# Differential attention with the matrix engine's order written out by hand, and the projections spread over all its items

## The chip, the cores and the metric

One core of one Trainium2 chip runs the kernel. The metric is device time in microseconds (us) from start to end of one execution; lower is better. A core has a matrix engine (TensorE, PE in the rows; PEld is its weight load), VectorE (DVE), ScalarE (ACT), GpSimd (POOL) and SyncE (SP), which here issues the weight transfers. Each engine works through its own queue in order and waits on semaphores for the others.

## What is computed

The reference is a four-layer block followed by a two-layer block over 256 tokens of width 1024. The change lies in layer 1 of the first block, a differential attention with 8 heads over 256 latent and 256 context tokens:

```python
def diff_attend(q1, q2, k1, k2, v, lam):
    scale = DIFF_HEAD_DIM ** -0.5
    s1 = jnp.einsum("bqhd,bkhd->bhqk", q1, k1).astype(jnp.float32) * scale
    s2 = jnp.einsum("bqhd,bkhd->bhqk", q2, k2).astype(jnp.float32) * scale
    p = jax.nn.softmax(s1, axis=-1) - lam * jax.nn.softmax(s2, axis=-1)
    return jnp.einsum("bhqk,bkhe->bqhe", p.astype(v.dtype), v)
...
q, k, v = jnp.split(h @ w_qkv, 3, axis=-1)      # rotary positions on the latent q and k
...
return (rms_norm(o, subln_g) * (1 - lam_init)).reshape(b, s, D_MODEL) @ w_o
```

Latent queries see all 512 keys, context queries the 256 context keys. A residual addition, a norm and an MLP of hidden width 4096 follow, as in every layer.

## The kernel before, in words

All products run on TensorE in pieces of a high and a low part, so one projection product is three matmuls. `loadw` fetches 256 columns of a weight (1 MB), and ScalarE (L306) and VectorE (L307) split them into two halves of high and low parts; five such halves fit at a time.

The attention of `diff` is cut into 24 items (h, it): for each of 8 heads two blocks of 128 latent queries (it = 0, 1) and one item with both context blocks (it = 2). An item has four parts:

- `scores`: ScalarE and VectorE split the queries (L396, L397); TensorE makes both score maps (L1227); VectorE takes maxima (L1231) and negates them (L1233); ScalarE takes the exponentials (L1238); VectorE combines the two maps into the probabilities p (L1242, L1243, L1247). From the second head on, the keys of the next head are split in the item with it = 2.
- `values`: TensorE transposes p (L1258), ScalarE copies the transpose out (L1260, tile `pt`), TensorE multiplies it with the values (L1267), ScalarE copies and squares the result (L1269, L1272). With it = 2 VectorE then computes the head's norm (L415 to L421) and scales the output (L1281).
- `finish`, once for each head: TensorE transposes the output (L1288), ScalarE and VectorE split it (L1290, L1291).
- fill: `qkv(g)` makes keys, queries and values of the head pair g in 8 steps, first four over 512 columns (`linear`, L324, L325, L327), then four over 256 columns (`val`, L1199 to L1201), each of 24 matmuls. `wo` is half of the output projection as `linear_k` with 8 steps of 12 matmuls over 512 columns (L351 to L353); step k needs the finished head k. The other half follows in `tail`.

The program traces, for each item, `scores` of this item, then steps of the fill, then `values` of the item before (`pipe_feed`). The fill of pair g+1 runs during the six items of pair g, so the last pair's six items have no projections left and take `wo` in the portions of DIFF_WO. The order in which each engine issues is not the traced one: the framework's scheduler reorders all instructions by readiness in its own model, with the traced order as priority.

`rows_add(rate)` adds to a counter and, whenever it passes 1, traces one more unit of the modulation weights of later layers: a transfer of 1 MB and two or four VectorE reductions over it (L588). RATES[1] is its rate for each item of `diff`; RATES[2] and RATES[4] are those of the MLPs of layers 1 and 2. The units come in a fixed sequence, so those that `diff` does not take are taken by these MLPs.

Of the kernel before, what the change touches and what calls it, by code (L numbers as in the profile page):

```python
# [17 lines left out]
P = 128  # L18
# [208 lines left out]
}  # L227
NDT = 5
AHEAD = 200
RATES = (0.35, 0.13, 0.6, 0.0, 0.3)  # L230
START = 12
LEAD = 2
DIFF_WO = (0, 1, 1, 1, 1, 0, 3)
DIFF_FIN = ((0, 1), (2, 3), (4,), (5,), (6,), ())
ORDER = [2, 5, 8, 11, 0, 1, 3, 4, 6, 7, 9, 10] + list(range(12, 24))
SCHED = ((6, 0), (6, 0), (6, 0), (6, 0), (6, 1), (4, 3), (0, 2), (0, 2))
BOTH = [(0, 0, NL), (1, NL, NF)]
# [4 lines left out]
class Body:  # L242
# [27 lines left out]
    def mm(self, cols=512):  # L270
        return self.ps.tile([P, 512], F32, tag="mm", name=self.nm("mm"))
# [67 lines left out]
    def linear_k(self, aps, xs, n, evac, m0=0):  # L339


        mm = self.nc.tensor.matmul
        ns = n if isinstance(n, list) else [n] * 2 * len(aps)
        ws = [self.loadw(ap, 8, 256) for ap in aps]
        pss = [self.mm() for _ in range(2 * len(aps))]
        for k in range(8):
            for i, ps in enumerate(pss):
                w = ws[i // 2]
                c0 = (i % 2) * P
                n = ns[i]  # L350
                mm(ps[:, :n], w(0, k, c0, c0 + P), xs[k][0][:, :n], start=k == 0, stop=False)  # L351
                mm(ps[:, :n], w(0, k, c0, c0 + P), xs[k][1][:, :n], start=False, stop=False)
                mm(ps[:, :n], w(1, k, c0, c0 + P), xs[k][0][:, :n], start=False, stop=k == 7)  # L353
            if k < 7:
                yield
        for i, ps in enumerate(pss):
            evac(m0 + i, ps)
        yield

    def pipe_begin(self, a, b, lag):  # L360

        self.pp = (a, b, lag, [])
# [795 lines left out]
    def diff(self, mod, nxt):  # L1158
        nc = self.nc
# [49 lines left out]
        def keys(h):  # L1209
            kx[h] = self.split(ks.pop(h)[:, :512])  # L1210

        def scores(h, it):


            self.rows_add(RATES[1])
            nq, k0, nk = (1, 0, 512) if it < 2 else (2, 256, 256)
            if h == 0 and it == 0:
                keys(0)
            q = self.split(qs[h][:, it * P:(it + nq) * P])
            if it == 2 and h < 7:  # L1220
                keys(h + 1)
            s = [self.aux(), self.aux()]
            for c in range(nq):
                for n_, (a, b) in enumerate(((0, 0), (0, 1), (1, 0))):
                    for i in range(2):
                        r = slice(64 * i, 64 * i + 64)
                        nc.tensor.matmul(s[i][:, c * nk:c * nk + nk], q[a][r, c * P:c * P + P],  # L1227
                                         kx[h][b][r, k0:k0 + nk], start=n_ == 0, stop=n_ == 2)
            mx, nm, ac, r = [self.sm(4)[:, :2 * nq] for _ in range(4)]
            for i in range(2):  # L1230
                nc.vector.tensor_reduce(out=mx[:, i * nq:i * nq + nq], in_=s[i].rearrange("p (c k) -> p c k", c=nq),  # L1231
                                        axis=AX.X, op=ALU.max)
            nc.vector.tensor_scalar(out=nm, in0=mx, scalar1=-scale, scalar2=None, op0=ALU.mult)  # L1233
            es = [self.g() for _ in range(2)]
            c0 = 4 * h + it
            for i in (1, 0):
                for c in range(nq):
                    nc.scalar.activation(es[i][:, c * nk:c * nk + nk], s[i][:, c * nk:c * nk + nk], AF.Exp,  # L1238
                                         bias=nm[:, i * nq + c:i * nq + c + 1], scale=scale,
                                         accum_out=ac[:, c:c + 1] if i else dac[:, c0 + c:c0 + c + 1])  # L1240

            nc.vector.reciprocal(r[:, :nq], ac[:, :nq])  # L1242
            nc.vector.scalar_tensor_tensor(out=r[:, :nq], in0=r[:, :nq], scalar=nlam, in1=dac[:, c0:c0 + nq],  # L1243
                                           op0=ALU.mult, op1=ALU.mult)
            for c in range(nq):
                sl = slice(c * nk, c * nk + nk)
                nc.vector.scalar_tensor_tensor(out=es[0][:, sl], in0=es[1][:, sl], scalar=r[:, c:c + 1],  # L1247
                                               in1=es[0][:, sl], op0=ALU.mult, op1=ALU.add)
            return es[0]

        def values(h, it, p):


            g, e0 = h // 2, (h % 2) * P
            nq = 1 if it < 2 else 2
            ps = self.aux()
            for j in range(4):
                nc.tensor.transpose(ps[:, j * P:j * P + P], p[:, j * P:j * P + P], self.ident)  # L1258
            pt = self.g()[:, :512]
            nc.scalar.copy(pt, ps)  # L1260
            if it == 0:
                of[h] = self.g()[:, :512]
            o = self.aux()
            nj = 4 // nq
            for j in range(4):
                jk = j if it < 2 else 2 + j % 2
                nc.tensor.matmul(o[:, j // nj * P:j // nj * P + P], pt[:, j * P:j * P + P],  # L1267
                                 vs[g, jk // 2][:, jk % 2, e0:e0 + P], start=j % nj == 0, stop=j % nj == nj - 1)
            nc.scalar.copy(of[h][:, it * P:(it + nq) * P], o[:, :nq * P])  # L1269
            sq = self.tp.tile([P, 512], F32, tag="sq", name=self.nm("sq"), bufs=2)  # L1270
            for c in range(nq):
                nc.scalar.activation(sq[:, c * P:c * P + P], o[:, c * P:c * P + P], AF.Square,  # L1272
                                     accum_out=dss[:, 4 * h + it + c:4 * h + it + c + 1])
            if it == 2:
                hc = slice(4 * h, 4 * h + 4)
                ep = self.sm(4)
                nc.vector.scalar_tensor_tensor(out=ep, in0=dac[:, hc], scalar=EPS, in1=dac[:, hc],
                                               op0=ALU.mult, op1=ALU.mult)
                self.rstd_of(dss[:, hc], dr[:, hc], 1.0 / P, ep)
                o3 = of[h].rearrange("p (q e) -> p q e", e=P)  # L1280
                nc.vector.tensor_tensor(out=o3, in0=o3, in1=dr[:, hc].unsqueeze(2).to_broadcast([P, 4, P]), op=ALU.mult)  # L1281

        def finish(h):

            ps = self.aux()
            o = of.pop(h)
            for j in range(4):
                nc.tensor.transpose(ps[:, j * P:j * P + P], o[:, j * P:j * P + P], self.ident)  # L1288
            hi, lo = self.pair(512)
            nc.scalar.activation(hi, ps, AF.Copy, scale=sg)  # L1290
            nc.vector.scalar_tensor_tensor(out=lo, in0=ps, scalar=sg, in1=hi.bitcast(F32), op0=ALU.mult,  # L1291
                                           op1=ALU.subtract)
            os_[h] = (hi, lo)
# [4 lines left out]
        def qkv(g):  # L1298
            yield from kq(g)
            yield from val(g)  # L1300
# [9 lines left out]
        hs = self.nb.hs  # L1310
        yield from val(0)
        wo = self.linear_k([I["diff_w"][12], I["diff_w"][13]], os_, 512, out)
        for g in range(4):
            items = [(h, it) for h in (2 * g, 2 * g + 1) for it in range(3)]
            fill = qkv(g + 1) if g < 3 else wo
            if g == 0:
                self.pipe_begin(scores, values, 1)
            if g < 3:
                self.pipe_feed(items, fill, 4 / 3)
                self.drain(fill)  # L1320
            else:
                for i, it in enumerate(items):
                    self.pipe_feed([it], wo, DIFF_WO[i])
                    for h in DIFF_FIN[i]:
                        finish(h)
            yield
        self.pipe_end(wo, 0)
        for _ in range(DIFF_WO[6]):
            next(wo)
        finish(7)  # L1330
        self.drain(wo)
        yield from self.tail([I["diff_w"][12 + u] for u in (2, 3)], [os_[h] for h in range(8)], out, 4)

    def mla(self, streams, mod, nxt):
# [87 lines left out]
        def scores(h, qi):  # L1422
            self.rows_add(RATES[3])
            s = self.aux()
# [123 lines left out]
    def first(self):  # L1548
        nc, I = self.nc, self.I
        with ExitStack() as ctx:  # L1550
# [23 lines left out]
            for l in range(DEPTH):  # L1574
# [38 lines left out]
                def ev(m, ps, st=None, mod=mod, streams=streams, n=n, l=l):  # L1613
# [5 lines left out]
                    elif st:  # L1619
                        self.final_add(m)  # L1620

                mlp = self.mlp_gen([I["mlp_w1"][l, u] for u in range(16)], w2, n, ev, nxt_mix if l < 3 else None)
                self.run(mlp, (RATES[0], RATES[2], RATES[4], 0)[l], START,
                         self.mod_units([20, 21, 22, 23], mod) if l == 0 else iter(()))
# [613 lines left out]
```

## Time and profile before

| what | value |
|---|---|
| median of 3 runs | 2950.53 us (2950.01 to 2952.84) |
| the profiled execution | 2948.07 us |
| its span, first to last instruction | 2946.3 us |
| TensorE busy | 2863.0 us, 97% of the span, 20316 matmuls |
| VectorE busy | 2153.2 us, 73% |
| ScalarE busy | 1489.9 us, 51% |
| mean granted TensorE clock | 0.991 |

The page's busy share of TensorE counts the modelled duration of pipelined matmuls, so a share near 100% says that one always was in flight, not that they followed each other as closely as they can. How close they came is read from the distance of their starts.

### The profile page before, as it was taken

The numbers are of one execution on the slowest core, as the hardware profiler recorded it, in microseconds if no ns is written. First come the engines' busy times: TensorE is split into PE (matmuls) and PEld (weight loads), VectorE is DVE, ScalarE is ACT, GpSimd is POOL, SyncE is SP. The second block draws the span as 40 slices with busy tenths as digits, with TensorE's granted clock in tenths as the row PEclk, the third lists the DMA queues.
The fourth block names the chain that finished last, engine by engine and source line by source line (L and its number), as shares of the span: only waits on it lengthen the run. The fifth ranks groups of instructions, "written<-read, shape, count | busy, mean of one in ns | idle before, by whom it ended". The sixth has DMA issues, their size and how long they took to land.

```text
span 2946.3 us, 51090 instructions
## 1 busy us (share of the span) xinstructions
PE 2863.0 (97%) x20316; PEld 2593.5 (88%) x20316; DVE 2153.2 (73%) x4707; ACT 1489.9 (51%) x2941; POOL 18.0 (1%) x66
## 2 busy tenths in 40 slices
PE   8999999998999999999999999999999999999999
PEld 6788889886888888599999999988999999989999
DVE  5597667775986667677756789886666799886765
ACT  5433323554432334855555567655554567655553
POOL 1000000000000000000000000000000000000000
PEclk9999999999999999999999999999999999999999
DMA  9454443320375553145525534333444444333553
GB/s 343 172 200 159 170 160 135 115 87 15 129 284 214 205 196 108 43 169 205 199 99 191 184 138 160 132 115 115 146 172 173 146 156 144 129 116 130 185 186 129
DMA packets 70366, 460.81 MB, mean 156 GB/s; under 512 B 7792, under 2 KB 9840, under 8 KB 16752
## 3 DMA queue, kind: packets, MB, share of 16 engines
q1 hardware_dynamic: 69984, 456.51, 43.6%
q8 instruction: 160, 2.62, 0.4%
q10 hardware_dynamic: 144, 1.05, 0.1%
q14 instruction: 78, 0.64, 0.1%
HBM read 456.47 MB, written 1.05 MB: 155 GB/s over the span
## 4 chain that ended last, share of the span: by engine, by line
PE 85%; DVE 8%; ACT 4%; DMA 1%; issue 1%; ACTq 0%; SPq 0%; DVEq 0%
PE mm L324 23%; PE mm L325 23%; PE mm L327 22%; DVE wlo L307 2%; ACT whi L306 1%; PE mm L675 1%; PE mm L674 1%; PE mm L676 1%; PE aux L1267 1%; PE mm L745 1%; PE aux L545 1%; PE mm L746 1%; PE mm L744 1%; DVE t L1701 1%; PE aux L1227 1%
## 5 line engine op out<-in xcount | busy, mean ns | idle before, releaser
L324 PE MATMUL mm<-g,whi 128*128 128x256 f32 (+3 forms) x5008 | 1406.9, 310 | 12.9 <-DVE t L1701 6.0
L325 PE MATMUL mm<-g,whi 128*128 128x256 f32 (+3 forms) x5008 | 1400.4, 308 | 0.5 <-DVE g L397 0.5
L306 ACT CAST whi<-raw 128x1024 fp32r<-128x1024 f32 (+2 forms) x670 | 697.5, 1048 | 821.0 <-PE mm L325 723.7
L324 PEld LDWEIGHTS mm<-g,whi 128*128 128x128 f32 x5008 | 941.6, 188 | 75.6 <-issue 15.7
L325 PEld LDWEIGHTS mm<-g,whi 128*128 128x128 f32 x5008 | 941.3, 188 | 51.7 <-issue 3.1
L307 DVE TENSOR_TENSOR wlo<-raw,whi 128x1024 fp32r<-128x1024 f32 (+2 forms) x670 | 809.5, 1210 | 122.0 <-ACT whi L306 65.7
L327 PE MATMUL mm<-g,wlo 128*128 128x256 f32 (+3 forms) x5008 | 835.2, 308 | 0.0
L327 PEld LDWEIGHTS mm<-g,wlo 128*128 128x128 f32 x5008 | 712.8, 188 | 47.0 <-issue 0.7
L588 DVE CUSTOM_DVE_ANT_0 junk<-raw,silu_b 128x1024 bf16<-128x1024 f32 x208 | 253.8, 1220 | 46.8 <-DMA raw<-in_mod_wT 44.9
L607 DVE SCALAR_TENSOR_TENSOR x<-mm,mod,x 128x256 f32<-128x256 f32 x216 | 98.3, 479 | 129.1 <-PE mm L327 125.4
L769 DVE TENSOR_TENSOR y<-mm,rb 128x256 f32<-128x256 f32 (+1 forms) x144 | 61.3, 427 | 89.8 <-PE mm L327 68.5
L846 DVE TENSOR_TENSOR g<-t,g 128x256 fp32r<-128x256 f32 (+2 forms) x192 | 98.5, 514 | 4.2
L843 ACT ACTIVATE t<-t 128x256 f32<-128x256 f32 (+2 forms) x192 | 94.0, 491 | 8.0 <-DVE g L846 2.9
L1701 DVE SCALAR_TENSOR_TENSOR t<-mm,cwh,t 128x270 f32<-128x270 f32 (+2 forms) x192 | 91.9, 490 | 2.7 <-ACT t L1698 2.4
L2195 DVE TENSOR_TENSOR x<-x,mm 128x272 f32<-128x272 f32 (+1 forms) x64 | 27.5, 429 | 81.0 <-PE mm L327 81.0
L675 PE MATMUL mm<-g,whi 128*128 128x256 f32 x240 | 66.7, 287 | 1.7 <-DVE g L643 1.6
L676 PE MATMUL mm<-g,wlo 128*128 128x256 f32 x240 | 65.5, 282 | 0.0
L841 ACT ACTIVATE t<-mm 128x512 f32<-128x512 f32 x64 | 37.9, 600 | 53.7 <-PE mm L327 53.6
L845 DVE CAST g<-t 128x256 fp32r<-128x256 f32 (+2 forms) x192 | 64.0, 334 | 1.3 <-ACT t L843 0.9
L674 PE MATMUL mm<-g,whi 128*128 128x256 f32 x240 | 60.7, 285 | 2.6 <-ACT g L642 2.6
L744 PE MATMUL mm<-g,whi 128*128 128x258 f32 (+2 forms) x192 | 54.5, 287 | 1.0 <-ACT g L716 0.7
L745 PE MATMUL mm<-g,whi 128*128 128x258 f32 (+2 forms) x192 | 54.7, 286 | 0.3 <-DVE g L717 0.3
(409 smaller groups left out, 3270.9 us busy)
## 6 DMA issues: line engine op xcount, KB each, us to landing
raw<-in_mlp_w SPq DMA_DIRECT2D x128, 1024.0 KB, 4.9
raw<-in_w_in SPq DMA_DIRECT2D x76, 1024.0 KB, 4.9
raw<-in_mod_wT SPq DMA_DIRECT2D x72, 1024.0 KB, 4.9
raw<-in_w_up SPq DMA_DIRECT2D x32, 1024.0 KB, 4.8
raw<-in_w_dn SPq DMA_DIRECT2D x32, 1024.0 KB, 4.8
raw<-in_diff_w SPq DMA_DIRECT2D x16, 1024.0 KB, 4.8
raw<-in_w_sd SPq DMA_DIRECT2D x16, 1024.0 KB, 4.8
raw<-in_mod_w SPq DMA_DIRECT2D x13, 1024.0 KB, 5.3
```

The source lines that it names most:

```text
L306: nc.scalar.copy(hi, v)
L307: nc.vector.tensor_tensor(out=lo, in0=v, in1=hi.bitcast(F32), op=ALU.subtract)
L324: mm(ps, w(0, k, c0, c1), xs[k][0], start=first and k == 0, stop=False)
L325: mm(ps, w(0, k, c0, c1), xs[k][1], start=False, stop=False)
L327: mm(ps, w(1, k, c0, c1), xs[k][0], start=False, stop=last and k == n - 1)
L588: nc.vector.tensor_tensor_reduce(out=self.junk, in0=r[:, D * j:D * j + D], in1=self.silu_b[:, D * s:D * s + D], scale=1.0, scalar=0.0, op0 ...
L607: self.nc.vector.scalar_tensor_tensor(out=self.x[m][:, c0:c1], in0=ps[:, c0:c1], scalar=mod[:, gc * 8 + m, s:s + 1], in1=self.x[m][:, c0:c ...
L675: mm(pss[i][:, c0:c1], w(0, k, o, o + P), l, start=False, stop=False)
L676: mm(pss[i][:, c0:c1], w(1, k, o, o + P), h, start=False, stop=k == 7)
L843: nc.scalar.activation(s[:, :n], t[:, :n], AF.Square)
L846: nc.vector.tensor_tensor(out=lo, in0=s[:, :n], in1=hi.bitcast(F32), op=ALU.subtract)
L1701: nc.vector.scalar_tensor_tensor(out=t[:, sft:L2], in0=ps[:, :L2 - sft], scalar=cw[:, 3 - sft:4 - sft], in1=t[:, sft:L2], op0=ALU.mult, op ...
```

## The change

On TensorE, every matmul and transpose that is traced inside the new block `with self.in_order()` keeps its traced place behind the one before. Inside it, one loop over all 24 items traces, for item i: the transposes of item i-1 (`turned`, which now holds the transposes and the copy `pt`), the scores of item i, the value products of item i-1, and then the fill of item i. The fills of the three remaining head pairs are one chain of 24 steps, given out by DIFF_QKV over the items 0 to 18; the items 3, 5, 9, 11, 16 and 17 get a single `val` step, the item 18 two. `wo` gets one step after each of the items 19 to 22 and two after 23, one after the last value product, and the last after the last `finish`. RATES[1] falls from 0.13 to 0.05. No arithmetic changes.

```diff
-RATES = (0.35, 0.13, 0.6, 0.0, 0.3)
+RATES = (0.35, 0.05, 0.6, 0.0, 0.3)
...
-DIFF_WO = (0, 1, 1, 1, 1, 0, 3)
-DIFF_FIN = ((0, 1), (2, 3), (4,), (5,), (6,), ())
+DIFF_FIN = ((0,), (1, 2), (3,), (4,), (5,), (6,))
+DIFF_QKV = (1, 2, 1, 1, 2, 1) * 2 + (1,) * 6 + (2,)
...
+    def in_order(self):
+
+        nc, keep = self.nc, self.tc.keep_in_program_order
+        ctx = ExitStack()
+        for nm_ in ("matmul", "transpose"):
+            f = getattr(nc.tensor, nm_)
+            setattr(nc.tensor, nm_, lambda *a, f=f, **k: keep(f(*a, **k)))
+            ctx.callback(delattr, nc.tensor, nm_)
+        return ctx
...
-        def values(h, it, p):
-
-
-            g, e0 = h // 2, (h % 2) * P
-            nq = 1 if it < 2 else 2
+        def turned(h, it, p):
+
             ps = self.aux()
             for j in range(4):
                 nc.tensor.transpose(ps[:, j * P:j * P + P], p[:, j * P:j * P + P], self.ident)
             pt = self.g()[:, :512]
             nc.scalar.copy(pt, ps)
+            return pt
+
+        def values(h, it, pt):
+
+
+            g, e0 = h // 2, (h % 2) * P
+            nq = 1 if it < 2 else 2
...
-        for g in range(4):
-            items = [(h, it) for h in (2 * g, 2 * g + 1) for it in range(3)]
-            fill = qkv(g + 1) if g < 3 else wo
-            if g == 0:
-                self.pipe_begin(scores, values, 1)
-            if g < 3:
-                self.pipe_feed(items, fill, 4 / 3)
-                self.drain(fill)
-            else:
-                for i, it in enumerate(items):
-                    self.pipe_feed([it], wo, DIFF_WO[i])
-                    for h in DIFF_FIN[i]:
+
+
+        items = [(h, it) for h in range(8) for it in range(3)]
+        fill = self.chain(*(qkv(g) for g in (1, 2, 3)))
+        last = None
+        with self.in_order():
+            for i, it in enumerate(items):
+                pt = turned(*last) if last else None
+                p = scores(*it)
+                if last:
+                    values(*last[:2], pt)
+                last = (*it, p)
+                j = i - 18
+                for _ in range(DIFF_QKV[i] if i < 19 else 0):
+                    next(fill)
+                if j >= 0:
+                    if j > 0:
+                        next(wo)
+                    for h in DIFF_FIN[j]:
                         finish(h)
-            yield
-        self.pipe_end(wo, 0)
-        for _ in range(DIFF_WO[6]):
             next(wo)
-        finish(7)
-        self.drain(wo)
+            values(*last[:2], turned(*last))
+            next(wo)
+            finish(7)
+            self.drain(wo)
+        yield
```

## Rows read from the trace of the kernel before

**Rows 1.** Windows: stretch, its length, busy time of each engine, granted clock, DMA.

```profile
533.60:680.60 147.00, 145.59 (x925) 121.96 (x924) 110.01 (x299) 80.31 (x238) 0.00 (x0) 1.00 0.24 86
680.60:745.54 64.94, 49.86 (x261) 37.23 (x261) 34.18 (x98) 28.64 (x89) 0.00 (x0) 0.89 0.05 17
```

**Rows 2.** Waits of TensorE, 500 to 780 us: total, times, longest.

```profile
PE aux L1267 <- ACT g L1260: 9.7, 8, 4.5
```

**Rows 3.** Timeline of TensorE at the longest wait (in brackets: idle before, releaser).

```profile
681.53 0.66 PE L1258 MATMUL aux<-k,g 128*128 128x128 f32 x4
686.68 2.08 PE L1267 MATMUL aux<-g,g 128*128 128x128 f32 x8 [4.49 <-ACT g L1260]
```

**Rows 4.** Timeline of ScalarE in the same wait.

```profile
686.04 0.58 ACT L1260 COPY g<-aux 128x512 f32<-128x512 f32 x1
```

**Rows 5.** Timeline of TensorE, last 24 us of the attention.

```profile
732.24 0.60 PE L1258 MATMUL aux<-k,g 128*128 128x128 f32 x4
733.51 1.16 PE L1267 MATMUL aux<-g,g 128*128 128x128 f32 x8 [0.67 <-ACT g L1260]
738.64 1.09 PE L1288 MATMUL aux<-k,g 128*128 128x128 f32 x4 [3.97 <-DVE g L1281]
740.51 2.08 PE L351 MATMUL mm<-g,whi 128*128 128x512 f32 x4 [0.78 <-ACT g L1290]
```

**Rows 6.** Timeline of TensorE, an item in the dense stretch.

```profile
640.16 1.05 PE L1267 MATMUL aux<-g,g 128*128 128x128 f32 x8
641.14 0.96 PE L1227 MATMUL aux<-g,g 64*128 64x512 f32 x6
...
643.52 2.03 PE L327 MATMUL mm<-g,wlo 128*128 128x512 f32 x8
645.39 0.60 PE L1258 MATMUL aux<-k,g 128*128 128x128 f32 x4
645.74 0.47 PE L324 MATMUL mm<-g,whi 128*128 128x512 f32 x1
```

**Rows 7.** Timeline of TensorE, first and last of 96 matmuls over 256 columns.

```profile
522.21 0.28 PE L1199 MATMUL mm<-whi,g 128*128 128x256 f32 x1
...
533.41 0.28 PE L1201 MATMUL mm<-whi,g 128*128 128x256 f32 x1
```

**Rows 8.** Timeline of TensorE: scores of the items 3, 17, 19, 21 and 22.

```profile
559.12 0.96 PE L1227 MATMUL aux<-g,g 64*128 64x512 f32 x6
...
673.97 1.20 PE L1227 MATMUL aux<-g,g 64*128 64x256 f32 x12
...
691.84 1.06 PE L1227 MATMUL aux<-g,g 64*128 64x512 f32 x6
...
709.24 1.06 PE L1227 MATMUL aux<-g,g 64*128 64x512 f32 x6
...
717.27 0.98 PE L1227 MATMUL aux<-g,g 64*128 64x512 f32 x6
```

**Rows 9.** Timeline of VectorE: the probabilities of the same five items.

```profile
564.77 0.74 DVE L1247 SCALAR_TENSOR_TENSOR g<-g,sm,g 128x512 f32<-128x512 f32 x1
...
679.04 0.88 DVE L1247 SCALAR_TENSOR_TENSOR g<-g,sm,g 128x256 f32<-128x256 f32 x2
...
696.86 0.75 DVE L1247 SCALAR_TENSOR_TENSOR g<-g,sm,g 128x512 f32<-128x512 f32 x1
...
713.64 0.75 DVE L1247 SCALAR_TENSOR_TENSOR g<-g,sm,g 128x512 f32<-128x512 f32 x1
...
722.33 0.75 DVE L1247 SCALAR_TENSOR_TENSOR g<-g,sm,g 128x512 f32<-128x512 f32 x1
```

**Rows 10.** Window of L588 alone: busy on VectorE, clock, DMA.

```profile
533.60:680.60 147.00, 9.81 (x16) 1.00 0.24 86
```

**Rows 11.** Window in the MLP of layer 1, columns as in the first group.

```profile
800.00:820.00 20.00, 20.00 (x88) 16.25 (x87) 19.97 (x37) 9.68 (x15) 0.00 (x0) 1.00 0.71 259
```

**Rows 12.** The page's costliest groups: busy, mean ns of one, idle before.

```profile
L306 ACT CAST whi<-raw 128x1024 fp32r<-128x1024 f32 (+2 forms) x670 | 697.5, 1048 | 821.0 <-PE mm L325 723.7
```

## The prediction, made before the changed kernel ran

> **What bounds the kernel now.** TensorE is busy 97% of the span, so I looked for the places where it is not, in windows. Layer 1's attention, with its first scores at 533.6 us and its last `wo` matmul before 745.54, falls into two stretches [rows 1]. In the first (items 0 to 17, all projections) TensorE idles 147.00 - 145.59 = 1.4 us at the full clock. In the second (items 18 to 23, only `wo` as fill) it idles 64.94 - 49.86 = 15.1 us, and the granted clock averages 0.89. The list of waits names the first cause [rows 2]: value products wait for ScalarE's copy of the transposes, 9.7 us in 8 waits. The timeline of the end shows the second: the last `finish` waits 3.97 us for VectorE [rows 5]. The longest wait shows the mechanism [rows 3, 4]: the transposes are issued at 681.53, but ScalarE copies only at 686.04, though nothing but the transposes feeds that copy. It is traced behind the exponentials of the *next* item, so it queues behind a whole softmax, and with no projections left TensorE has nothing else.
>
> **Prices.** Distances of starts, not durations, price a full-clock TensorE. Value products take 641.14 - 640.16 = 0.98 us, transposes 645.74 - 645.39 = 0.35, scores at most their 0.96, and eight matmuls over 512 columns 645.39 - 643.52 = 1.87, so 0.234 each [rows 6]. Over 256 columns it is (533.41 - 522.21) / 95 = 0.118 [rows 7]. A 512-column step (24 matmuls) is 5.61 us, a `val` step 2.83, a `wo` step (12) 2.81.
>
> Softmax latency, from the start of the scores to the end of the combination: 564.77 + 0.74 - 559.12 = 6.4 us (item 3), 679.04 + 0.88 - 673.97 = 5.9 (item 17), 713.64 + 0.75 - 709.24 = 5.15 (item 21, few neighbours on VectorE) [rows 8, 9]. The items 3, 5, 9, 11, 16 and 17 have 5.8 to 6.8, mean 6.25; those two are the first and last of the six.
>
> **First stretch, part by part.** The new order makes each item transposes, next scores, values, fill, transposes. The transposes now need a softmax that began with the scores, and everything behind them waits too: the next scores, values and projections stand in the same queue. The cover is scores 0.96 + values 0.98 + fill, plus some 0.2 of handovers (145.59 busy less 140 us of priced work gives 0.3 an item). A 512-column step makes 7.75: longer than 6.8, no wait. A single `val` step makes 4.97: a wait of 6.25 - 4.97 = 1.3 us, six times, 7.8 us. Bounds: latency 5.15 gives 0.2 each (1.2 in all), 6.8 gives 1.8 (11). The value products need the copy 733.51 - 732.24 = 1.27 us after the transposes' start [rows 5]; in between stand transposes and scores, 0.35 + 0.96. So nothing is lost when ScalarE is free; it is busy 80.3 of 147 us [rows 1], so I take 0.1 an item, 1.7 in this stretch, with bounds 0 and 0.5. The stretch loses two `val` steps (to item 18) and one item's transposes and values: 5.66 + 1.33. Sum: 147.00 - 1.4 - 7.0 + 7.8 + 1.7 = 148.1 us.
>
> **Second stretch.** Item 18: transposes, scores, values, two `val` steps, one `finish` (0.35) = 8.3; the two steps cover its softmax, which was the 4.49 us wait. Items 19 to 22: 0.35 + 0.96 + 0.98 + 2.81 + 0.35 = 5.45 each, one `finish` more: 22.15. Their cover, 5.1 + 0.2, against their latencies leaves 0.45 each, 1.8: the four have a mean of 5.75, with 696.86 + 0.75 - 691.84 = 5.8 for item 19 and 722.33 + 0.75 - 717.27 = 5.8 for item 22 as first and last [rows 8, 9] (bounds 0 and 4). Item 23: 5.45 + 2.81 = 8.26, no wait. The end: transposes 0.35, wait 0.92, values 0.98; then the chain that took 738.64 - 733.51 - 0.98 = 4.15 us [rows 5] now runs over one `wo` step, so 2.81 and a wait of 1.34; `finish` and its split 1.5 (1.87 before, partly at the lower clock); the last step 2.81: 10.71. With handovers 0.3 x 6 and copies 0.1 x 6: 8.3 + 22.15 + 1.8 + 8.26 + 10.71 + 2.4 = 53.6 us against 64.94.
>
> This uses full-clock prices throughout. Before, the clock falls after the long waits: the same eight value products take 2.08 us at 686.68 and 1.16 at 733.51 [rows 3, 5], and the last `wo` step 745.54 - 740.51 = 5.0 instead of 2.81. With no wait above 1.5 us I expect that back, about 4 us of the gain. [...]
>
> **The rate.** 24 x 0.08 = 1.9, so two modulation units move from here to the MLP of layer 1, and two from there to that of layer 2. Here they occupy VectorE, 9.81 us for two [rows 10]; I count no gain, since TensorE barely waits for it now. In MLP 1, VectorE is already full between 800 and 820 us, and TensorE shows no idle time there [rows 11]: the weights split ahead cover it. A unit of four reductions is 4.9 us, one of two half of that, so two heavier units add 4.9 us. Bounds 0 and 5; I take 0.5. In MLP 2 the same amount is spread thinner: nothing. Weight transfers keep their order and only come later in the items; DMA is 24% busy here [rows 1].
>
> **Sum.** 148.1 + 53.6 = 201.7 against 211.94: 10.2 less, 9.7 with the rate. The profiled execution, 2948.07, becomes 2938.4; it lies 2.5 under the median of the runs, and taken from that the prediction is 2950.53 - 9.7 = 2941 us. All low bounds together give about 2930, all high ones about 2961.
>
> **Rivals.**
> 1. *No wait is exposed.* With less on VectorE and the copy ahead of the exponentials, every softmax is as quick as item 21's. The waits shrink from 7.8 to 1.2 and from 1.8 to 0, the copies' 2.3 vanish: 10.5 better, about 2931. For it: two heavy reduction units go, which stood among these softmaxes. Against: the weight splits and rotary operations on VectorE stay, and the mean of six was 6.25.
> 2. *A wash.* The six `val` items wait as long as their slowest (11 us), the last step stays at the lower clock (2.2), MLP 1 pays for its units (5): 3.4 + 2.2 + 4.5 worse, about 2951, no change. For it: the dense stretch idles only 1.4 us today, because the scheduler may slip projections in wherever a softmax is late, and that freedom is given up.
> 3. *Slower: the copy.* One mechanism: ScalarE is inside a weight cast (L306, 1.05 us [rows 12]) or queues one ahead of the copy, so that each of the 24 value groups waits, now with all projections locked behind it. At 0.5 us each it takes back 24 x 0.4 = 9.6, the whole gain; from 0.75 the kernel is over 0.2% slower, and a full cast each time gives 2941 + 23 = 2964. For it: these copies are the largest wait today. Against: today they queue behind exponentials traced before them, which the new tracing puts after them.
>
> **How the numbers follow.** 0.2%, 5.9 us, is about what can be told from no change. Forecast, gain 4 to 14 us: 0.55 (of this 0.08 under 5.9). Rival 1: 0.13. Rival 2, with everything from a gain of 4 to a loss of 6: 0.24. Rival 3 or a like loss: 0.08. Faster 0.47 + 0.13 = 0.60, same 0.32, slower 0.08. The predicted time is the forecast's, 2941; its own range is 2936 to 2947. For 8 in 10 the range reaches to rival 1's end, 2931, and over the wash to 2952.
>
> **What would show it.** Right: the second stretch near 54 us with no wait above 1.5 us and a clock near 1.00; in the first, short waits of transposes (L1258's successor) for the combination L1247, only in the items with one `val` step; value products that no longer wait for exponentials. Wrong: waits before transposes in 512-column items too; value products waiting for the copy everywhere; projections waiting for weights (L306, L307), which I price at nothing because five halves are held and transfers are far from full; or idle time appearing in the MLPs.

## The result, and the profile after

The changed kernel takes 2978.56 us (median, 2976.16 to 2981.08); the kernel before, beside it, 2951.69. The ratio is 1.0088 with a 95% interval of 1.0075 to 1.0101: slower, by some 26 us, where 2941 us and a gain were forecast. The two profiled executions lie 33 us apart (spans of 2946.3 and 2979.3): one is faster than the median of its kernel, the other slower.

The profiled executions say where. Layer 1's attention, from its first scores to the first L324 of the projection behind it, lasted 211.94 us before [rows 1]. These are the same two stretches after (items 0 to 17, then items 18 to 23 with `wo`), from the view of windows; columns as in [rows 1]:

```profile
533.41:715.33 181.92, 151.86 (x881) 123.22 (x881) 109.49 (x290) 80.26 (x239) 0.00 (x0) 0.95 0.16 58
715.33:775.92 60.59, 51.22 (x305) 40.69 (x306) 36.11 (x100) 30.37 (x88) 0.00 (x0) 0.97 0.05 18
```

The first stretch grew by 34.9 us, though 44 of its matmuls (925 - 881) moved to the second, and TensorE idles in it 181.92 - 151.86 = 30.1 us where it idled 1.4. The second, with these 44 more, shrank by 4.3 of the 11.3 that were forecast. What lies behind the attention took 2979.3 - 775.92 = 2203.4 us against 2946.3 - 745.54 = 2200.8. So the loss sits in the stretch that was dense. The waits of TensorE over both stretches (total, times, longest):

```profile
PE aux L366 <- ACT g L406: 30.5, 23, 2.0
PE aux L366 <- DVE g L407: 2.4, 4, 1.3
PE aux L366 <- DVE g L1257: 2.3, 5, 0.5
PE aux L366 <- DVE g L1295: 1.1, 1, 1.1
PE mm L366 <- ACT g L1304: 0.8, 1, 0.8
PE aux L366 <- ACT g L1267: 0.7, 1, 0.7
```

L366 is the wrapper that holds the order, so every ordered matmul carries its number; the tile tells which it is. One row stands out: 23 waits, 1.3 us each, for L406. That is neither the probabilities (L1257) nor the copy `pt` (L1267), the two waits that the prediction priced; it is ScalarE's cast in `split`, which makes the high part of the *next* item's queries. That is about once an item. One of them, in item 13, in the timeline of TensorE:

```profile
668.04 0.60 PE L366 MATMUL aux<-k,g 128*128 128x128 f32 x4
670.36 2.42 PE L366 MATMUL aux<-g,g 64*128 64x512 f32 x14 [1.72 <-ACT g L406]
```

The transposes are issued at 668.04; the scores (the first six of the x14) start at 670.36, 2.32 us later, where 0.35 was counted on. ScalarE in that time:

```profile
669.25 0.37 ACT L1193 COPY g<-mm 128x256 f32<-128x256 f32 x1 [1.83 <-DVE t L1154]
669.51 0.59 ACT L1267 COPY g<-aux 128x512 f32<-128x512 f32 x1
669.99 0.31 ACT L406 CAST g<-g 128x128 fp32r<-128x128 f32 x1
```

Read the idle time in the first line: ScalarE did nothing for 1.83 us. It was then first to evacuate the projection step just ended (L1193, which waits until VectorE has read the same tile for the rotary product, L1154), then to copy `pt`, and only then to cast queries that had been in memory for several items. The cast is 0.31 us of work on data that was ready; it is late because it is third in a queue whose head must wait for the end of the projection.

### The profile page after: what moved, and what is told of

Same layout as the page of the kernel before. It is cut to its first block, busy times and chain, and to the rows that moved or that the text cites. A ratio compares the mean times of both kernels' runs of the same rounds, so it can differ in the third digit from the quotient of the medians.

```text
span 2979.3 us, 51093 instructions
## 1 busy us (share of the span) xinstructions
PE 2872.1 (96%) x20316; PEld 2600.1 (87%) x20316; DVE 2157.3 (72%) x4707; ACT 1489.7 (50%) x2941; POOL 18.0 (1%) x66
## 3 DMA queue, kind: packets, MB, share of 16 engines
q10 hardware_dynamic: 144, 1.05, 0.1%
HBM read 456.47 MB, written 1.05 MB: 154 GB/s over the span
## 4 chain that ended last, share of the span: by engine, by line
PE 85%; DVE 9%; ACT 4%; issue 1%; DMA 1%; POOL 0%; ACTq 0%; POOLq 0%; DVEq 0%
PE mm L324 22%; PE mm L325 22%; PE mm L327 22%; PE mm L366 3%; DVE wlo L307 3%; PE aux L366 2%; PE mm L685 1%; PE mm L684 1%; PE mm L686 1%; PE mm L755 1%; PE mm L756 1%; ACT whi L306 1%; PE mm L754 1%; PE aux L555 1%; PE aux L1959 1%
## 5 line engine op out<-in xcount | busy, mean ns | idle before, releaser
L324 PE MATMUL mm<-g,whi 128*128 128x256 f32 (+4 forms) x4912 | 1369.1, 308 | 13.3 <-DVE t L1722 6.1
L325 PE MATMUL mm<-g,whi 128*128 128x256 f32 (+4 forms) x4912 | 1363.3, 307 | 1.1 <-DVE g L407 0.9
L324 PEld LDWEIGHTS mm<-g,whi 128*128 128x128 f32 (+1 forms) x4912 | 924.7, 189 | 70.2 <-issue 13.0
L325 PEld LDWEIGHTS mm<-g,whi 128*128 128x128 f32 (+1 forms) x4912 | 923.8, 188 | 48.4 <-issue 2.9
L327 PE MATMUL mm<-g,wlo 128*128 128x256 f32 (+3 forms) x4912 | 810.6, 306 | 0.0
L327 PEld LDWEIGHTS mm<-g,wlo 128*128 128x128 f32 x4912 | 694.9, 188 | 42.9 <-issue 0.7
L366 PE MATMUL aux<-g,g 128*128 128x128 f32 (+2 forms) x384 | 58.8, 354 | 34.5 <-ACT g L406 30.5
L366 PEld LDWEIGHTS aux<-g,g 64*128 64x128 f32 (+1 forms) x384 | 41.6, 203 | 52.0 <-ACT g L406 35.9
L366 PE MATMUL mm<-g,whi 128*128 128x512 f32 x256 | 71.8, 416 | 1.1 <-ACT g L1304 0.8
L685 PE MATMUL mm<-g,whi 128*128 128x256 f32 x240 | 66.6, 286 | 2.0 <-DVE g L653 2.0
```

What stands on the lines that cost most here:

```text
L324: mm(ps, w(0, k, c0, c1), xs[k][0], start=first and k == 0, stop=False)
L325: mm(ps, w(0, k, c0, c1), xs[k][1], start=False, stop=False)
L327: mm(ps, w(1, k, c0, c1), xs[k][0], start=False, stop=last and k == n - 1)
L366: setattr(nc.tensor, nm_, lambda *a, f=f, **k: keep(f(*a, **k)))
L685: mm(pss[i][:, c0:c1], w(0, k, o, o + P), l, start=False, stop=False)
```

## Experiments

The theory going in (A): the loss is this queue position, `turned`, then the split inside `scores`, with all of TensorE locked behind it. Rivals were the fixed order as such, the new tracing, and the lower rate of row sums (D). In the table, the stretches are those of the two windows above, in each run's profiled execution; "behind" is the span less the end of the attention. Ratios are to the kernel before in the same set of runs; its own median differs by up to 2.6 us between the sets, so a difference between kernels of two sets is given as a span, from the ratios and from the medians. Where the portions or the order differ, some matmuls change stretch (before, 925 stand in the first, after 881), so between kernels the sum of the two columns compares more safely than either.

| kernel | median us | ratio [95%] | items 0-17 | items 18-23 | behind |
|---|---|---|---|---|---|
| before | 2949 to 2952 | 1 | 147.0 | 64.9 | 2200.8 |
| after | 2978.56 | 1.0088 [1.0075, 1.0101] | 181.9 | 60.6 | 2203.4 |
| e1 after, split ahead | 2947.91 | 0.9998 [0.9989, 1.0007] | 153.2 | 54.0 | 2206.9 |
| e2 after, free order | 2946.86 | 0.9996 [0.9987, 1.0006] | 151.6 | 58.4 | 2206.8 |
| e3 before, rate 0.05 | 2952.82 | 1.0010 [1.0001, 1.0020] | 148.1 | 65.2 | 2203.6 |
| e4 before, fixed order | 2991.33 | 1.0147 [1.0132, 1.0162] | 184.4 | 70.2 | 2205.5 |
| e5 e1, rate 0.13 | 2947.32 | 0.9991 [0.9981, 1.0002] | 155.9 | 54.0 | 2202.3 |
| e6 e1, L1193 on VectorE | 2942.45 | 0.9975 [0.9957, 0.9994] | 152.0 | 54.0 | 2203.5 |
| e7 e5, order from item 18 | 2939.30 | 0.9962 [0.9948, 0.9976] | 145.6 | 56.7 | 2206.2 |
| e8 e5 and e6 | 2944.93 | 0.9982 [0.9971, 0.9992] | 155.0 | 53.9 | 2206.9 |
| e9 e7 and e6 | 2942.63 | 0.9970 [0.9959, 0.9980] | 144.6 | 55.1 | 2209.6 |
| e10 e7, rate 0.05 | 2940.82 | 0.9964 [0.9950, 0.9977] | 145.0 | 54.0 | 2205.9 |
| e11 e7, free order | 2938.30 | 0.9957 [0.9942, 0.9973] | 145.5 | 54.0 | 2205.9 |
| e12 after, split on GpSimd | 2955.23 | 1.0015 [1.0004, 1.0025] | 159.7 | 57.1 | 2199.1 |
| e13 before, split ahead | 2943.33 | 0.9972 [0.9962, 0.9983] | 145.4 | 59.8 | 2203.9 |
| e14 e2, rate 0.13 | 2949.89 | 1.0000 [0.9991, 1.0009] | 156.6 | 57.6 | 2200.5 |

### What costs the time: e1, e2, e3, e4, e12

**e1, the split traced one item earlier**, so that it stands ahead of the projection's evacuation:

```diff
+            q = queries(*items[0])
             for i, it in enumerate(items):
                 pt = turned(*last) if last else None
-                p = scores(*it)
+                p = scores(*it, q)
+                if i < 23:
+                    q = queries(*items[i + 1])
```

(`queries` holds the split of an item's queries and, with it = 2, that of the next head's keys; the rest of the edit only moves these lines out of `scores`.)

> The changed kernel with one thing moved: the split of the next item's queries (and keys) is traced right after the scores of the item before, so that ScalarE holds it behind the exponentials and no longer behind the copy of the transposes. Theory A (in the fixed order the next scores wait for the query split, which ScalarE only reaches after the copy of the transposes; some 1.4 us for each of 23 items): the scores no longer wait for ScalarE's split, and the time falls by 27 to 35 us from the changed kernel's 2978.6, to 2943 to 2952. Theory B (the fixed order as such: the projections are locked behind whatever wait comes next, so the value products or the transposes wait instead): within 10 us of 2978.6.

Measured 2947.91, 27 to 31 us below the changed kernel, with the same order on TensorE. The wait for L406 is gone from TensorE's list (lines shift by four):

```profile
PE aux L366 <- ACT g L1271: 8.3, 14, 1.6
PE aux L366 <- DVE g L1261: 3.2, 6, 1.0
```

and transposes and scores stand together; the timeline of TensorE and ScalarE in an item like the one above:

```profile
645.97 0.60 PE L366 MATMUL aux<-k,g 128*128 128x128 f32 x4
646.50 0.96 PE L366 MATMUL aux<-g,g 64*128 64x512 f32 x6
647.01 0.37 ACT L1193 COPY g<-mm 128x256 f32<-128x256 f32 x1 [1.66 <-DVE t L1154]
647.28 0.59 ACT L1271 COPY g<-aux 128x512 f32<-128x512 f32 x1
647.92 1.16 PE L366 MATMUL aux<-g,g 128*128 128x128 f32 x8 [0.47 <-ACT g L1271]
```

The scores now follow after 0.53 us. What is left is the next thing in the same queue: the copy `pt` behind the same evacuation, 0.47 us here, 8.3 in all.

**e2, the changed kernel without the fixed order** (`with self.in_order():` left out).

> The changed kernel without the fixed order on TensorE: the same tracing order, the same portions of projections, the same rate, but the scheduler places the matmuls. Theories A and B: the projections fill the gap between transposes and scores again, 2940 to 2955. Theory C (the tracing order or the portions are bad in themselves, on ScalarE and VectorE as well): 2965 or more.

2946.86: the new tracing alone costs nothing that can be told. Free to choose, the scheduler lets TensorE go on with projections while the split is late: TensorE waits 0.9 us in all for L406 there. **e3, the rate alone** on the kernel before (RATES[1] = 0.05):

> The kernel before with only RATES[1] lowered from 0.13 to 0.05. Theories A to C: within 4 us of the kernel before. Theory D (the modulation units moved into the MLPs make these wait for VectorE): 5 to 20 us slower than the kernel before.

1.0010, at most some 6 us and not where the loss is. **e4, the fixed order alone**, around the tracing of before:

> The kernel before with TensorE kept in its traced order over all 24 items: scores, projections, transposes and value products of the item before, at the old rate and portions. Theory A: here the transposes and the value products that need their copy stand next to each other, so that each of 24 items waits 0.9 to 1.5 us for the copy and little for the split, which the value products cover: 2970 to 2990, with waits of the value products in place of the scores. Theory C (the new tracing is what costs): 2945 to 2960.

2991.33, the slowest of all and 1 us over the range expected. Here the copy is traced behind the exponentials of the next item, and with the order locked it becomes the first cost; the split, which was expected to be covered, is the second (TensorE's waits over the attention):

```profile
PE aux L366 <- ACT g L1270: 28.4, 24, 4.0
PE aux L366 <- ACT g L406: 12.7, 12, 1.5
```

L1270 is the copy `pt` there. So the order needs an operand early, and what it costs depends on where ScalarE's queue has that operand.

**e12, the split at its old place, on another engine.** e1 moved the split in time; this moves it only to an empty queue.

```diff
-            q = self.split(qs[h][:, it * P:(it + nq) * P])
+            q = self.split(qs[h][:, it * P:(it + nq) * P], nc.gpsimd)
```

> The changed kernel, with its tracing order untouched, but the query split (cast and difference) on GpSimd, whose queue is empty, in place of the scalar and the vector engine. Theory A in its sharp form (what waits is not the split but its place in the scalar engine's queue, behind the evacuation of the projection and the copy pt): the 30.5 us of waits for L406 go, and some 25 to 30 us of time with them: 2948 to 2954. Rival B (the split is late since its operands come late, or its buffers do, wherever it stands): 2970 to 2980, with the waits named after GpSimd instead. Rival G (GpSimd takes several us for each split, and the scores wait for it): between the two, 2955 to 2970, to be told by GpSimd's durations.

2955.23, 22 to 23 us better than the changed kernel. That is 1 us over the upper end of theory A and just inside the range of rival G, in which TensorE waits for a slow GpSimd. The durations and the waits decide between them. GpSimd needs longer for each split than ScalarE and VectorE did, but 0.5 + 0.7 us and not several (its two groups of instructions: busy, mean ns). It does not matter, because its queue lets it start early: the cast for the scores at 684.58 us starts at 669.34. No matmul waits for its splits any more, and the weight loads wait 0.2 us once:

```profile
L410 POOL TENSOR_TENSOR g<-g,g 128x128 fp32r<-128x128 f32 (+1 forms) x24 | 17.5, 730 | 1.9
L409 POOL CAST g<-g 128x128 fp32r<-128x128 f32 (+1 forms) x24 | 11.5, 479 | 623.6 <-ACT whi L306 468.0 <-PE aux L366 73.6 <-DVE g L1260 24.1
```

```profile
PE aux L366 <- DVE g L1260: 9.2, 7, 2.0
PE aux L366 <- ACT g L1270: 8.4, 12, 1.3
```

That settles it: not the split's work, its place in the queue. What remains there of waits is mainly the combination (L1260) and the copy (L1270).

### Where the forecast gain went: e5 to e11

With the split ahead, items 18 to 23 take 54.0 us, as forecast, and yet e1 ends level with before. The first stretch is 6 us longer than before, with 44 matmuls fewer in it, and in this trace so is what lies behind the attention. Three ideas were tried: the rate put back (e5), the raw half in `ev_rope` copied by VectorE, so that `pt` no longer stands behind it (e6), and the fixed order only where work is short (e7).

```diff
-                nc.scalar.copy(t[:, 256:512], ps[:, 256:512])
+                nc.vector.tensor_copy(t[:, 256:512], ps[:, 256:512])
```

```diff
+                if i == 18:
+                    fixed.enter_context(self.in_order())
```

> e1 with the rate of the row sums back at 0.13 (RATES[1]); the rest of the change stays. In e1 attention ended 5.6 us earlier than before (first L324 of the projection behind it at 739.95 against 745.54 us), but what lies behind it took some 6 us longer. Theory R (the row sums that the low rate leaves over are done behind attention, where the tensor engine has no gaps, as the run with the rate alone showed with +3.7 us): 2944 to 2946 us, some 2 to 4 us below e1, with the stretch behind attention back at 2200 to 2203 us. Rival S (the stretch behind attention is longer for another reason, such as weight loads that start later): within 1.5 us of e1. Rival T (the added row sums open new waits between the fixed steps): above e1.

> e1 with the copy of the raw half in the evacuation of keys and queries (L1193) on the vector engine instead of the scalar engine. In e1 the copy of the transposed weights (pt) stands behind this copy in the scalar engine's queue, which waits for the second step of the rope (21.6 us in 12 waits); the value products behind it wait 8.3 us in 14 waits. Theory C (the first stretch, 153.2 us in e1 against 148.1 predicted and 147.0 before, is longer because the copy pt sits behind that evacuation): some 4 to 6 us below e1, 2942 to 2944 us, and the waits for the copy pt fall to under 4 us. Rival V (the vector engine becomes late by 12 copies of 0.4 us, and the reductions of the scores with it): no gain, 2947 to 2950. Rival N (the value products wait 1.3 us in any case for the round through the copy, with whatever stands before it): 2946 to 2948.

> e5 with the fixed order only from item 18 on, so that the scheduler's own order stands where projections of 8 output tiles cover every item, and the fixed order where it is short of work. If the gain of the fixed order is that of the last six items alone (64.9 us before, 54.0 in e1) and the scheduler does better in the first stretch (147.0 before, 153.2 in e1): 2937 to 2942 us, 5 to 9 us below e1. Rival (the scheduler's own tracing of the new order is no better than the fixed one in the first stretch, as the free run of the new tracing, 2946.9, may say): 2944 to 2948. The window of items 0 to 17 tells them apart: 147 or 153 us.

> e5 and e6 together: rate 0.13 and the raw half copied by the vector engine, the whole stretch in the fixed order. If both theories (R: -3 us, C: -5 us) hold and add up: 2939 to 2942 us. If only one holds: 2943 to 2946. If the vector engine is late (12 more copies and 24 more times 0.08 row sums of it): 2946 or more.

e5 gave 0.6 us by the medians and 2 by the ratios, less than the intervals: theory R is not shown. In its trace the stretch behind the attention is back at 2202.3, as R said, but the row sums lengthen the first stretch by 2.7 us (155.9). e6 gave 5.5 us in the median, and the waits for the copy fell as theory C said, but the waits for VectorE rose in their place (the list of waits, e6):

```profile
PE aux L366 <- DVE g L1261: 4.9, 7, 2.3
PE aux L366 <- DVE rt L430: 2.7, 1, 2.7
PE aux L366 <- DVE rt L429: 1.9, 1, 1.9
PE aux L366 <- ACT g L1271: 1.8, 4, 0.7
```

and the first stretch itself is only 1.2 us shorter; with the old rate (e8) the same edit gives 2.4 us in the median and 0.9 in the stretch, where both theories together would have given 2939 to 2942. So theory C holds for the wait, and for the time only in part. e7 fits its theory: the scheduler's own order brings the first stretch back to 145.6 us. It is not as dense as before: with 44 matmuls fewer TensorE idles 145.60 - 140.81 = 4.8 us in it, against 1.4. Here are its windows:

```profile
534.67:680.27 145.60, 140.81 (x881) 116.02 (x880) 109.48 (x299) 78.98 (x238) 0.00 (x0) 1.00 0.25 87
680.27:736.93 56.66, 52.10 (x305) 42.01 (x305) 34.66 (x99) 30.10 (x88) 0.00 (x0) 0.94 0.06 20
```

Then e7 was varied: with e6's edit (e9), with the low rate (e10), and without any fixed order (e11, the two added lines left out).

> The fixed order for the last six items alone, as in e7 (2939.3), and the raw half of keys and queries copied by the vector engine, as in e6. In e7 the first stretch (145.6 us) is already dense and the copy pt costs it 1.4 us of waits, so what e6 repaired is hardly there: 2937 to 2941 us, no difference from e7 that can be told. Rival: the scheduler plans by its own costs and places the vector engine's copies so that reductions come late: 2941 to 2945.

> e7 with the low rate of row sums, 0.05. By the run with the rate alone (+3.7 us) this is 2942 to 2944; by the pair e5 and e1 (0.6 us apart, in the fixed order) it is the same as e7, 2938 to 2941: the row sums take as long behind attention as in it.

> e7 without any fixed order: what the order of the last six items is worth, with the split ahead and the spread projections in place. If the order is what shortens the last six items (64.9 us before, 58.4 in the free run of the new tracing, 54 to 56.7 with the order): 58 to 62 us there and 2942 to 2946 in all. Rival (the spread projections and the split ahead do it, and the order nothing): within 1.5 us of e7.

e9 and e10 can't be told from e7, though the median of e9 lies in the range of its rival. e11 is the surprise, and its rival was right: with no fixed order at all, items 18 to 23 take 54.0 us and the whole 2938.30, as fast as any kernel here. Its windows:

```profile
534.64:680.17 145.53, 143.00 (x900) 118.37 (x900) 109.49 (x299) 78.89 (x238) 0.00 (x0) 1.00 0.25 86
680.17:734.18 54.01, 49.60 (x286) 38.77 (x286) 32.80 (x97) 28.36 (x86) 0.00 (x0) 0.97 0.06 20
```

The order of TensorE, which the change is about, is thus worth nothing that can be told in the last six items and costs 8 us or so in the others (e5 against e7).

### Which part brings the gain then: e13, e14

e13 is the kernel before with the split ahead and nothing else; e14 is e11 with the split back at its old place.

> The kernel before with one edit: the split of the next item's queries (and keys) is traced behind the scores of the item before. All else, order and rate too, is as before. Theory P (the early copy of the transposed weights and the spread projections shorten the last six items, and the split ahead adds to it): little gain here, 2946 to 2950 us, the last six items still 62 us or more, with value products waiting for the copy behind the exponentials. Theory Q (the late split alone kept the scores, and with them everything, late before as well): most of the gain of the kernel with the split ahead in a free order (2938.3) is here already: 2938 to 2942.

> The changed kernel without the fixed order and with the rate 0.13: it differs from the kernel with the split ahead in a free order (2938.3) by the split's place alone. If the split's place matters in a free order too, some 2944 to 2947 us, as the free run with the rate 0.05 had (2946.9); if that run was slower for its rate alone, 2938 to 2941.

e13 is 0.9972 [0.9962, 0.9983] of before, between its two expectations; e14 is 1.0000, its median above both of its own. So the new tracing alone gives nothing, the split alone some 8 us, both together 11 to 13. Whether the tracing adds to the split can't be told for sure: the intervals of e13 and e11 overlap. The windows of e13 and, below, of e14:

```profile
531.88:677.24 145.36, 144.56 (x926) 121.90 (x925) 107.92 (x299) 80.45 (x238) 0.00 (x0) 1.00 0.24 87
677.24:737.06 59.82, 47.97 (x261) 37.60 (x261) 33.78 (x99) 28.71 (x89) 0.00 (x0) 0.89 0.05 18
```

```profile
533.41:690.04 156.63, 149.90 (x929) 122.04 (x928) 112.90 (x301) 81.22 (x241) 0.00 (x0) 0.98 0.25 88
690.04:747.59 57.55, 49.41 (x257) 37.54 (x258) 32.93 (x97) 26.84 (x85) 0.00 (x0) 0.86 0.00 1
```

The kernel before already paid for the late split, without a wait that names it: its scores start when ScalarE gets to the cast, and TensorE fills the time with projections while it has them. These two rows of the timeline of ScalarE *before* belong to the scores at 673.97 and 691.84 [rows 8], which start 0.46 and 0.76 us after them:

```profile
673.51 0.93 ACT L396 CAST g<-g 128x256 fp32r<-128x256 f32 x2
...
691.08 0.29 ACT L396 CAST g<-g 128x128 fp32r<-128x128 f32 x1
```

In e13 the casts of the same two items stand 2.83 and 4.24 us before their scores (670.61 and 686.68):

```profile
667.78 0.92 ACT L396 CAST g<-g 128x256 fp32r<-128x256 f32 x2
...
682.44 0.29 ACT L396 CAST g<-g 128x128 fp32r<-128x128 f32 x1
```

In e13's second stretch the longest wait of value products for `pt` is still there, 4.48 us as against 4.49 [rows 3], and the clock still averages 0.89; but the stretch is 5.1 us shorter. The wait, in e13's timeline of TensorE:

```profile
683.27 2.08 PE L1278 MATMUL aux<-g,g 128*128 128x128 f32 x8 [4.48 <-ACT g L1271]
```

## Why the prediction was wrong, point by point

**The step that failed** is the cover: "each item transposes, next scores, values, fill", with "in between stand transposes and scores, 0.35 + 0.96. So nothing is lost when ScalarE is free". It priced the scores as if their operands were there. The split of the queries (L396, L397) was described among the parts of `scores` but given neither a row nor a term, although the new tracing puts it directly behind the copy `pt`. The missing term is measured: 30.5 + 2.4 = 32.9 us. The waits for the probabilities came only where the prediction put them, before the transposes of items with a single fill step (5, 9, 11, 16, 17 and 22), but at 0.3 to 0.5 us each. They make 2.7 us (2.3 for L1257, and 0.4 in item 9 that is named after the norm, L425) where 7.8 + 1.8 were added: the softmaxes were shorter than before, 5.2 us in item 16 against the mean of 6.25. The copy's 2.3 came out at 0.7. Net: 32.9 - 6.9 - 1.6 = 24 us, which would have made the forecast 2965.

The other 13 us or so are mostly not waits: for the same 881 matmuls in the first stretch TensorE is busy 151.86 us after, at a granted clock of 0.95, and 141.85 us in e1, at 0.99. Of these 10 us the clock makes some 8, as an estimate (0.05 x 181.92 - 0.01 x 153.17 = 7.6); no run tells where the rest comes from, nor what let the clock fall where it did.

**The first stretch**, 148.1 us forecast, measured 181.9. Even with the split ahead (e1) it is 153.2. The value products wait 7.0 us there for the copy and not 1.7, the transposes 4.4 and not 7.8, and TensorE is busy 141.85 us where the sum implies 138.6. For the copy, 0.1 an item was too little for an engine busy 80 of 147 us whose queue holds an evacuation that must wait for VectorE.

**The second stretch**, 53.6 forecast, measured 60.6, of which 6.8 are waits for the split, and 54.0 with the split ahead. Its sum came out once that term was gone, but the order is not what it takes: e11 has the 54.0 without it. It takes the new tracing and the split ahead: the two stretches together have 211.9 us before, 214.2 with the new tracing alone (e14), 205.2 with the split ahead alone (e13), and 199.5 with both (e11), each in a single trace.

**The last step's clock.** The prediction expected full clock through the waits at the end. After, they are 1.10, 0.78 and 0.28 us, and most of the last `wo` step runs at half the pace (timeline of TensorE):

```profile
771.69 0.51 PE L366 MATMUL mm<-g,whi 128*128 128x512 f32 x1 [0.28 <-DVE g L1305]
772.04 0.45 PE L366 MATMUL mm<-g,wlo 128*128 128x512 f32 x1
772.28 1.06 PE L366 MATMUL mm<-g,whi 128*128 128x512 f32 x2
773.13 0.63 PE L366 MATMUL mm<-g,wlo 128*128 128x512 f32 x1
773.56 1.06 PE L366 MATMUL mm<-g,whi 128*128 128x512 f32 x2
```

Three matmuls take 773.56 - 772.28 = 1.28 us, 0.43 each; the granted clock there is 0.50, the lower level. In e1 the waits are 1.10, 0.78 and 0.29, the granted clock stays at 1.00, and the same matmuls stand 0.23 apart:

```profile
737.30 0.50 PE L366 MATMUL mm<-g,whi 128*128 128x512 f32 x1 [0.29 <-DVE g L1309]
737.64 0.40 PE L366 MATMUL mm<-g,wlo 128*128 128x512 f32 x1
737.87 0.62 PE L366 MATMUL mm<-g,whi 128*128 128x512 f32 x2
738.33 0.39 PE L366 MATMUL mm<-g,wlo 128*128 128x512 f32 x1
738.56 0.62 PE L366 MATMUL mm<-g,whi 128*128 128x512 f32 x2
```

So the last step at the lower clock, a term of rival 2 (2.2 us), came true in the one trace and not in the other, after the same waits; it was worth 775.92 - 771.69 - (739.95 - 737.30) = 1.6 us. What tells the two apart, no run shows.

**The rate**, priced at 0.5 us. e3 says 1.0010, which would be 3 to 4 us; e5 against e1 and e10 against e7 show no difference, and "behind" has a mean of 2204.6 us over the nine traces with 0.13 and 2204.2 over the seven with 0.05. A cost of 0 to 4 us stays open.

**The rivals.** Rival 3 had the right kind of mechanism, ScalarE's queue with all projections locked behind it, and nearly the right price for an item (1.05 us for a full cast, where the waits for the split make 32.9 / 24 = 1.4), but it named the copy behind a weight cast and not the split behind the copy, and it got 8 in 100. Its evidence against, that the new tracing puts the copy ahead of the exponentials, was true of the copy alone. Rival 2's remark that the scheduler's freedom to slip projections in is given up was right as well: e5 against e7 prices it at some 8 us once the split is out of the way, e2 against after at 27 to 32 with it. Two of the prediction's sums are off by little: by its own prices the work of the dense stretch is 18 x 0.96 + 17 x 1.33 + 12 x 5.61 + 12 x 2.83 = 141.2 us and not 140, and rival 2's 11 - 7.8 is 3.2 and not 3.4. Neither moves the forecast.

## What to carry to other kernels

When an order is written out for one engine, list for every instruction in it *each* operand, and find where that operand's last preparation stands in its own engine's queue: a cheap operation on data long ready is as late as the slowest thing traced ahead of it. A free order can hide such a lateness, so no wait need name it; compare the start of a consumer with the end of its operand's producer, also where TensorE is busy in between. And try the cheap repair, tracing the preparation an item earlier, before the order: here it alone gave some 8 us of the 9.7 that the whole change was to give.

## What was not expected of the hardware

**The clock did not follow the waits evenly.** In the changed kernel every 20 us of the first stretch have waits of the same kind and TensorE busy for 16 to 18 us, but the granted clock is below 1.00 only between 540 and 640 us (windows of 20 us from 540 on; the columns as above):

```profile
560.00:580.00 20.00, 16.52 (x86) 13.94 (x86) 14.80 (x41) 7.37 (x26) 0.00 (x0) 0.83 0.31 106
...
620.00:640.00 20.00, 16.27 (x90) 13.04 (x89) 10.43 (x25) 8.42 (x26) 0.00 (x0) 0.91 0.15 52
640.00:660.00 20.00, 16.14 (x132) 14.24 (x130) 11.62 (x34) 11.21 (x36) 0.00 (x0) 1.00 0.00 1
```

No run here explains the difference. **The stretch behind the attention**, whose code no experiment touched but for the rate, took 2199.1 to 2209.6 us in the sixteen profiled executions, a spread as large as most of the effects studied. The second stretch repeats better, with 53.9 to 54.0 us in six of the eight kernels that have the new tracing and the split ahead. So a few us between two single executions say little without the medians beside them.
